# A gated decoder block on eight cores: token-major GLU into the convolution, LN statistics and pooling on VectorE, and small stages run beside the dense matmuls

## The chip, the cores and the metric

One Trainium2 chip, all 8 cores. Each core computes 2048 of the 4 x 4096 tokens, plus a halo of 32 earlier tokens, with all the weights; no core talks to another. The metric is the device time of the slowest core, in microseconds (us). Five engines matter: TensorE (PE, matmuls and transposes), VectorE (DVE), ScalarE (ACT), GpSimd (POOL) and SyncE (SP, which here only starts loads and stores). In the traces of this case each engine works through its own list of instructions in the order of the program: one that waits holds up everything behind it on that engine (in the changed kernel GpSimd stood 20.59 us before one load, and the load behind it was issued only after that). TensorE's results land in PSUM, which the kernels use as eight banks of 512 columns; VectorE or ScalarE reads them out (an eviction) before the kernel uses a bank again, and PE waits where that is late. In a matmul, the stationary operand is the one loaded into the array first (PEld in the views, 98 ns a load in the changed kernel's MLP). L-numbers are lines of the kernel; many are lines of helpers.

There is a second, slower state: in five executions here the cores of one die show a mean granted TensorE clock of 0.81 to 0.95 where the other die has 0.97 to 0.99, and the run is 7 to 15% longer. Such runs are left out. The experiments were run in several sessions and on several chips: there, the median of the fast runs of the kernel before was between 1136 and 1140.4 us, so differences of 3 us between two kernels of different sessions mean little.

## The reference, cut to what matters

```python
u = rms_norm(h, mix_pre_g)
proj = u @ w_in                               # 1024 -> 5120: a, gate, p, two gates
a, gate = split(proj[..., :2048])
c = depthwise_causal_conv(a * sigmoid(gate))  # 31 positions, per channel
c = swish(layer_norm(c))                      # over the 1024 channels of a token
y_conv = c @ w_conv_out
z = trailing_mean(p, windows 2, 4, 8, 16) - p # one window per group of 256 channels
y_pool = (einsum(z, pool_w) * pool_scale) @ w_pool_out
h = h + rms_norm((g_conv * y_conv + g_pool * y_pool) @ w_o, mix_post_g)
v = square(relu(rms_norm(h, mlp_pre_g) @ w_ff1)) @ w_ff2       # 1024 -> 4096 -> 1024
out = h + rms_norm(v, mlp_post_g)
```

The dense products (GLU, pool projection, gated products, w_o, MLP) fill TensorE. The rest, that is norms, convolution, LN and pooling, is small, but the dense products depend on it.

## The kernel before

Every stage is finished before the next one begins. The convolution is done on TensorE, on groups of 8 channels by 16 positions, so the channel-major GLU result has to be transposed, regrouped, transposed again, multiplied and transposed back. LN sums are matmuls with a matrix of ones. The trailing means are matmuls with band matrices.

```python
def glu_group(cc, t0, n, blk):                 # channel-major: weights stationary
    for (po, sl, ...) in (a-half, gate-half):
        for kc in range(8):
            MM(po, sl[:, kc, ccl*128:(ccl+1)*128], uT[:, kc, t0:t0+n], kc == 0, kc == 7, ...)
    ACT(tmpA, pg, AF.Sigmoid, ...)
    TTOP("dve", u[:, cc, t0:t0+n], pa, tmpA, ALU.mult, ...)
# ... cut ...
for step in range(8 + 3):                      # the conv, a stage of its own
    if 0 <= step - 1 < 8: cv_t2(step - 1)      # second transposes + PSUM eviction
    if step < 8:          cv_t1(step)          # first transposes, also of the halo
    if 0 <= step - 3 < 8: cv_t3(step - 3)      # back to channel-major
    if 0 <= step - 2 < 8: cv_mm(step - 2)      # the 31 taps; then loads the next taps
# ... cut ...
for cc in range(8):                            # LN sums: ones-matmuls of s and s*s
    MM(ps[:, blk, :], onesb[:], s_t[:, cc, ...], ...)
    MM(ps[:, 4 + blk, :], onesb[:], sqb[:, sb, ...], ...)
# ... cut: pooling by band matrices pmb, then pool_w, then the two gated passes ...
for j in range(16):                            # w_o, a stage of its own
    ctx = s5_a(j)                              # load x again, 16 matmuls, squares
    if pend is not None: s5_b(*pend)           # residual, store, norm for the MLP
    pend = (j, ctx)
```

Of the kernel before, what the change touches and what calls it, by code (L numbers as in the profile page):

```python
# [10 lines left out]
AX = mybir.AxisListType  # L11

H = 32
NT = 2048
# [7 lines left out]
OFF_RA, RA_N = 0, 8 * TT  # L22
OFF_RB, RB_N = OFF_RA + RA_N, 8 * TT
OFF_RD, RD_N = OFF_RB + RB_N, 8 * NT
OFF_RW, RW_N = OFF_RD + RD_N, 8 * 2048
OFF_RC, RC_N = OFF_RW + RW_N, 8192
OFF_RDM, RDM_N = OFF_RC + RC_N, 8192
ARENA_N = OFF_RDM + RDM_N

class KB:  # L30
    ENG = ("pe", "act", "dve", "pool", "sp")
    N_DMA_SEM = 16

    def __init__(self, nc):
        self.nc = nc
        self.q = {e: [] for e in self.ENG}
        self.count = {e: 0 for e in self.ENG}
        self.last_write = {}
        self.readers = {}
        self.waited = {e: {} for e in self.ENG}  # L40
        self.dma_val = [0] * self.N_DMA_SEM
        self.dma_next = 0
        self.n_sw = 0
        self.ranges = {}

    def reg(self, name, start, n):
        self.ranges[name] = (start, start + n)
# [10 lines left out]
    def _clobbers(self, w):  # L58
        rg = self.ranges.get(w)
        if rg is None:  # L60
            return ()
        out = []
        for n2, (s2, e2) in self.ranges.items():
            if n2 != w and s2 < rg[1] and rg[0] < e2 and (n2 in self.last_write or n2 in self.readers):
                out.append(n2)
        return out

    def op(self, eng, fn, reads=(), writes=(), dma=False, after=()):
# [3 lines left out]
        writes = list(writes)  # L72
        extra = []
        for w in writes:
            extra.extend(self._clobbers(w))
        for r in reads:
            ev = self.last_write.get(r)
            if ev is not None:
                self._need(eng, ev, waits)
            if isinstance(r, tuple) and r[0] == "ps":  # L80
                for ev in self.readers.get(r, ()):
                    if ev[0] != eng:
                        self._need(eng, ev, waits)
        for w in writes + extra:
            ev = self.last_write.get(w)
            if ev is not None:
                self._need(eng, ev, waits)
            for ev in self.readers.get(w, ()):
                self._need(eng, ev, waits)
# [14 lines left out]
        for w in writes:  # L104
            self.last_write[w] = ev
            self.readers[w] = []
        for w in extra:
            self.last_write.pop(w, None)
            self.readers.pop(w, None)
        for r in reads:  # L110
            self.readers.setdefault(r, []).append(ev)
        return ev

    def final_wait(self, eng, resources):
        waits = {}
        for r in resources:
            ev = self.last_write.get(r)
            if ev is not None:
                self._need(eng, ev, waits)
        self.q[eng].append((waits, None, None, False))  # L120
# [28 lines left out]
def build_program(dbg=None):  # L149
# [8 lines left out]
    pool_w = din("pool_w", [4, 256, 256])  # L158
# [4 lines left out]
    vecs = din("vecs", [128, 32 + 248])  # L163
    gbd = din("gb", [4, DM])
    identd = din("ident", [128, 128])
    pmd = din("pm", [128, 4 * 288])
    convw = din("convw", [8, 128, 16 * 3 * 128])
    out = nc.dram_tensor("out", [NT, DM], F32, kind="ExternalOutput").ap()
    dbg_cv = nc.dram_tensor("dbg_cv", [128, 8 * NT], BF16, kind="ExternalOutput").ap() if dbg == "cv" else None

    with ExitStack() as es:
        T = lambda name, shape, dt: es.enter_context(nc.sbuf_tensor(name, shape, dt))
        arena = T("arena", [128, ARENA_N], BF16)
        xt = T("xt", [128, 2, DM], F32)
        xb = T("xb", [128, 3, DM], BF16)
        gb = T("gbt", [128, 2, DM], F32)
        tmpA = T("tmpA", [128, 4, 512], F32)
        stat = T("stat", [128, 4, 512], F32)
        sm = T("sm", [128, 64], F32)
        epst = T("epst", [128, 2], F32)  # L180
        vec = T("vec", [128, 32 + 248], F32)
        identf = T("identf", [128, 128], F32)
        identb = T("identb", [128, 128], BF16)
        onesb = T("onesb", [128, 128], BF16)
        pmb = T("pmb", [128, 4, 288], BF16)
        junkb = T("junkb", [128, DM], BF16)
        ps = es.enter_context(nc.psum_tensor("ps", [128, 8, 512], F32))
        kb = KB(nc)

        def aview(off, cnt, **dims):  # L190
            v = arena[:, off:off + cnt]
            if dims:
                names = list(dims)
                pat = "p (" + " ".join(names) + ") -> p " + " ".join(names)
                v = v.rearrange(pat, **{k: dims[k] for k in names[:-1]})
            return v

        uT = aview(OFF_RA, RA_N, k=8, t=TT)
        u = aview(OFF_RB, RB_N, k=8, t=TT)
        z_t = aview(OFF_RB, 8 * NT, k=8, t=NT)  # L200
        s_t = aview(OFF_RD, RD_N, k=8, t=NT)
        sqb = aview(OFF_RC, RC_N, b=2, t=NT * 2)
        Dm = aview(OFF_RDM, 2 * 31 * 128, b=2, j=31, q=128)
        m1 = aview(OFF_RC, RC_N + RDM_N, k=8, t=NT)
        ptm = aview(OFF_RC, 4 * 1024, b=4, n=1024)
        h1 = aview(OFF_RC, 16384, f=32, t=512)
        hT_all = stat[:].rearrange("p a n -> p (a n)").bitcast(BF16).rearrange("p (k t) -> p k t", k=8)

        def slot(i):
            return aview(OFF_RW + i * 2048, 2048, k=8, n=256)  # L210

        def wff1_off(c):
            return (OFF_RA + c * 4096) if c < 4 else (OFF_RD + (c - 4) * 4096)

        def wff1_blk(c):
            return aview(wff1_off(c), 4096, k=8, n=512)

        def wff2_off(f):
            return (OFF_RB + f * 1024) if f < 16 else (OFF_RW + (f - 16) * 1024)

        def wff2_fc(f):
            return aview(wff2_off(f), 1024)

        WO_SL = 0
        wo_t = aview(OFF_RW, 8192, h=2, k=8, n=512)

        for k in range(8):
            kb.reg(("uT", k, -1), OFF_RA + k * TT, H)
            for b in range(4):
                kb.reg(("uT", k, b), OFF_RA + k * TT + H + b * 512, 512)  # L230
            kb.reg(("u", k), OFF_RB + k * TT, TT)
            for b in range(4):
                kb.reg(("z", k, b), OFF_RB + k * NT + b * 512, 512)
            kb.reg(("s", k), OFF_RD + k * NT, NT)
            kb.reg(("m1", k), OFF_RC + k * NT, NT)
            kb.reg(("rw", k), OFF_RW + k * 2048, 2048)
            kb.reg(("wff1", k), wff1_off(k), 4096)
        for b in range(2):
            kb.reg(("sqb", b), OFF_RC + b * 4096, 4096)
            kb.reg(("Dm", b), OFF_RDM + b * 3968, 3968)  # L240
            kb.reg(("wo", b), OFF_RW + b * 4096, 4096)
        for b in range(4):
            kb.reg(("ptm", b), OFF_RC + b * 1024, 1024)
        for f in range(32):
            kb.reg(("wff2", f), wff2_off(f), 1024)
            kb.reg(("h1", f), OFF_RC + f * 512, 512)

        st = {"bank": 0, "k": 0, "alt": 0, "xi": 0, "ti": 0}

        def nb():  # L250
            b = st["bank"]
            st["bank"] = (b + 1) % 8
            return b

        def PSK(b):
            return ("ps", b)

        def alt():
            st["alt"] ^= 1
            return "act" if st["alt"] else "dve"  # L260

        def nti():
            st["ti"] = (st["ti"] + 1) % 4
            return st["ti"]

        def MM(out_ap, lhsT, rhs, start, stop, reads, writes):
            kb.op("pe", lambda e: e.matmul(out_ap, lhsT=lhsT, rhs=rhs, start=start, stop=stop), reads=reads, writes=writes)  # L267

        def TR(out_ap, in_ap, ident_ap, reads, writes):
            kb.op("pe", lambda e: e.transpose(out_ap, in_ap, ident_ap), reads=reads, writes=writes)  # L270

        def ACT(out_ap, in_ap, func, reads, writes, bias=None, scale=None, accum=None):
            kw = {}
            if bias is not None:
                kw["bias"] = bias
            if scale is not None:
                kw["scale"] = scale
            if accum is not None:
                kw["accum_out"] = accum
            kb.op("act", lambda e: e.activation(out=out_ap, in_=in_ap, func=func, **kw), reads=reads, writes=writes)  # L280

        def TTOP(eng, out_ap, in0, in1, op, reads, writes):
            kb.op(eng, lambda e: e.tensor_tensor(out=out_ap, in0=in0, in1=in1, op=op), reads=reads, writes=writes)  # L283

        def TS(eng, out_ap, in0, s1, op0, reads, writes):
            kb.op(eng, lambda e: e.tensor_scalar(out=out_ap, in0=in0, scalar1=s1, scalar2=None, op0=op0), reads=reads, writes=writes)
# [594 lines left out]
```

## Time and profile before

Three runs gave a median of 1137.19 us (1135.94 to 1138.77). The profiled execution spans 1134.0 us on its slowest core.

The page of the kernel before, parts 1 and 2: busy time of an engine with its share and instruction count, then PE's busy tenths in 40 equal slices of the span.

```profile
PE 1034.5 (91%) x6184; PEld 535.8 (47%) x6184; DVE 464.0 (41%) x696; ACT 380.0 (34%) x664; POOL 63.7 (6%) x76
...
PE   2999987788887999999997789999999999999997
```

PE looks 91% busy, but its low digits stand together: at the start, in slices 6 to 13 and in slices 22 to 24. A table of stretches makes this plain. The windows view of the kernel before, core 2; I chose the borders at the stages, and the columns are as the first line says (after the borders comes the length).

```profile
core 2: us, PE busy (x) PEld busy (x) DVE busy (x) ACT busy (x) POOL busy (x), PEclk, DMA share, GB/s
...
150.50:236.00 85.50, 65.08 (x1025) 61.02 (x1023) 47.22 (x69) 33.81 (x39) 6.93 (x11) 0.92 0.84 139
236.00:349.60 113.60, 93.80 (x864) 73.31 (x864) 89.86 (x119) 54.85 (x77) 5.89 (x7) 0.91 0.38 45
349.60:602.50 252.90, 251.73 (x1152) 113.08 (x1152) 73.32 (x107) 57.12 (x97) 38.03 (x39) 0.99 0.42 64
602.50:683.00 80.50, 59.70 (x272) 25.79 (x273) 42.80 (x76) 27.08 (x78) 0.00 (x0) 0.92 1.00 245
683.00:1127.00 444.00, 438.50 (x2096) 200.36 (x2096) 155.97 (x239) 124.11 (x246) 3.86 (x5) 1.00 0.25 69
```

| stretch (us) | stage | PE busy of | clock |
|---|---|---|---|
| 0 to 24.7 | start | 4.4 of 24.7 | 1.00 |
| 150.5 to 236 | conv | 65.1 of 85.5 | 0.92 |
| 236 to 349.6 | LN statistics, pool projection, pooling | 93.8 of 113.6 | 0.91 |
| 349.6 to 602.5 | products with `pool_w` (to about 366), both gated passes, the first four w_o tiles | 251.7 of 252.9 | 0.99 |
| 602.5 to 683 | the other w_o tiles, the first w_ff1 groups | 59.7 of 80.5 | 0.92 |
| 683 to 1127 | the rest of the MLP | 438.5 of 444.0 | 1.00 |

The gated products and the MLP leave almost nothing between matmuls (1.2 of 252.9 and 5.5 of 444.0 us): there, less matmul time is what is left to save, at 0.216 us per matmul of 512 columns. Conv, LN with pooling, and w_o wait, and their clock is lower as well (0.91 to 0.92). The waits view of the kernel before names what PE waited for (total us, number of waits, longest):

```profile
PE ps L267 <- ACT arena L280: 16.2, 8, 5.5
PE ps L270 <- DVE xb L289: 16.1, 10, 4.7
```

These are waits for PSUM evictions and transposes that wait for a norm; convolution weights that land late add 9.3 us.

### The profile page before, as it was taken

What the parts mean: (1) busy time and instruction counts of PE and PEld (TensorE: products, weight loads), DVE (VectorE), ACT (ScalarE), POOL (GpSimd) and SP (SyncE); (2) the same over time, 40 slices, a digit from 0 to 9 for tenths busy, and PEclk for the clock granted to TensorE, in tenths of its full rate; (3) what the DMA queues carried; (4) which work ended last, traced back from release to release, by engine and by line L of the source; (5) the groups of instructions that cost most, each with busy time, mean ns of one, the idle gap of its engine ahead of it and who ended that gap; (6) DMA issues with size and microseconds to landing.
All of it is one profiled execution on the core that took longest, in us unless ns stands there. A gap on an engine that the chain in (4) does not pass through costs nothing.

```text
span 1134.0 us, 17007 instructions; the slowest of 8 cores (1114.2 to 1134.0 us)
## 1 busy us (share of the span) xinstructions
PE 1034.5 (91%) x6184; PEld 535.8 (47%) x6184; DVE 464.0 (41%) x696; ACT 380.0 (34%) x664; POOL 63.7 (6%) x76
## 2 busy tenths in 40 slices
PE   2999987788887999999997789999999999999997
PEld 1454467647773444444443334444444444444443
DVE  3343245549796111232235456323332333234322
ACT  4677333314655211111124234222332233223211
POOL 2000000020000100122130001000000000000000
PEclk9999999889888999999999989999999999999999
DMA  9921079983007061193529998723102310131012
GB/s 204 161 67 57 1 120 165 164 104 47 1 1 130 8 85 21 28 147 36 87 22 217 233 260 189 138 82 99 43 1 65 109 51 1 56 112 38 1 55 75
DMA packets 60320, 98.71 MB, mean 87 GB/s; under 512 B 2480, under 2 KB 42672, under 8 KB 59216
## 3 DMA queue, kind: packets, MB, share of 16 engines
q0 software_dynamic: 46080, 46.96, 28.8%
q1 hardware_dynamic: 14160, 50.68, 13.5%
q8 instruction: 51, 0.84, 0.3%
q14 instruction: 29, 0.24, 0.1%
HBM read 127.81 MB, written 16.78 MB: 127 GB/s over the span
## 4 chain that ended last, share of the span: by engine, by line
PE 73%; DMA 14%; DVE 6%; ACT 3%; issue 3%; SPq 1%; POOL 0%; DVEq 0%; ACTq 0%; POOLq 0%
PE ps L267 70%; DMA arena<-xh 4%; DMA arena<-w_in 3%; DMA arena<-convw 3%; PE ps L270 3%; DMA xt<-xh 3%; DVE tmpA L283 2%; DVE gbt L293 1%; ACT arena L280 1%; DVE arena L299 1%; DMA xt<-out 1%; DVE xt L289 1%; DMA arena<-pool_w 1%; ACT junkb L280 1%; DVE arena L289 0%
## 5 line engine op out<-in xcount | busy, mean ns | idle before, releaser
L267 PE MATMUL ps<-arena 128*128 128x512 bf16 (+4 forms) x3936 | 732.4, 348 | 28.8 <-DMA arena<-convw 9.3
L267 PEld LDWEIGHTS ps<-arena 128*128 128x128 bf16 (+1 forms) x3936 | 364.9, 100 | 380.3 <-issue 45.5
L280 ACT ACTIVATE tmpA<-ps 128x512 f32<-128x512 f32 (+1 forms) x232 | 135.1, 583 | 354.1 <-PE ps L267 344.9
L267 PE MATMUL ps<-stat,arena 128*128 128x512 bf16 x1024 | 222.1, 379 | 8.9 <-ACT junkb L280 5.1
L267 PEld LDWEIGHTS ps<-stat,arena 128*128 128x128 bf16 x1024 | 99.6, 98 | 130.5 <-issue 11.4
L283 DVE TENSOR_TENSOR arena<-tmpA 128x512 bf16<-128x512 f32 x128 | 88.1, 692 | 113.9 <-ACT tmpA L280 113.8
L283 DVE TENSOR_TENSOR arena<-ps,tmpA 128x512 bf16<-128x512 f32 (+1 forms) x72 | 45.8, 636 | 146.6 <-ACT tmpA L280 141.6
L280 ACT ACTIVATE junkb<-ps 128x512 bf16<-128x512 f32 x64 | 37.9, 592 | 146.7 <-PE ps L267 93.6
L280 ACT ACTIVATE arena<-ps 128x512 bf16<-128x512 f32 (+5 forms) x71 | 50.9, 719 | 61.7 <-DVE arena L299 31.1
L283 DVE TENSOR_TENSOR tmpA<-ps,gbt 128x512 f32<-128x512 f32 x64 | 42.2, 686 | 61.6 <-ACT junkb L280 44.7
L293 DVE RECIPROCAL sm<-sm 128x1 f32<-128x1 f32 (+1 forms) x65 | 10.5, 161 | 115.8 <-ACT sm L280 115.8
L280 ACT ACT_TABLE_LOAD x32 | 41.1, 1283 | 46.6 <-DVE tmpA L283 14.6
L283 DVE TENSOR_TENSOR tmpA<-ps,tmpA 128x512 f32<-128x512 f32 x32 | 22.1, 692 | 75.6 <-ACT tmpA L280 75.6
L280 ACT ACTIVATE junkb<-xt 128x1024 bf16<-128x1024 f32 x26 | 27.4, 1053 | 68.7 <-DMA xt<-out 66.1
L270 PE MATMUL ps<-identb,xb 128*128 128x128 bf16 (+1 forms) x264 | 21.7, 230 | 30.3 <-DVE xb L289 16.1
L270 PE MATMUL ps<-identb,arena 128*128 128x128 bf16 (+2 forms) x640 | 39.1, 213 | 8.2 <-DVE arena L299 4.4
L299 DVE CAST arena<-ps 128x512 bf16<-128x512 f32 (+1 forms) x54 | 37.0, 686 | 13.9 <-PE ps L267 10.9
L270 PEld LDWEIGHTS ps<-identb,arena 128*128 128x128 bf16 (+2 forms) x640 | 35.2, 106 | 11.6 <-issue 9.5
L289 DVE SCALAR_TENSOR_TENSOR xt<-tmpA,sm,xt 128x1024 f32<-128x1024 f32 x24 | 30.8, 1285 | 14.4 <-DMA xt<-xh 11.1
L270 PEld LDWEIGHTS ps<-identb,xb 128*128 128x128 bf16 (+1 forms) x264 | 17.7, 103 | 40.0 <-issue 35.7
L289 DVE SCALAR_TENSOR_TENSOR xb<-xt,sm,gbt 128x1024 bf16<-128x1024 f32 x26 | 33.4, 1284 | 3.2 <-DVE sm L293 0.7
L299 DVE COPY arena<-ps 128x1024 bf16<-128x1024 bf16 (+2 forms) x46 | 27.8, 618 | 11.4 <-ACT arena L280 9.4
(44 smaller groups left out, 359.2 us busy)
## 6 DMA issues: line engine op xcount, KB each, us to landing
arena<-w_ff POOLq DMA_DIRECT2D x16, 1024.0 KB, 26.8
xt<-out SPq DMA_DIRECT2D x28, 512.0 KB, 4.0
arena<-convw POOLq DMA_DIRECT2D x8, 1536.0 KB, 14.3
out<-xt SPq DMA_DIRECT2D x24, 512.0 KB, 3.4
xt<-xh SPq DMA_DIRECT2D x20, 512.0 KB, 8.1
arena<-w_in POOLq DMA_DIRECT2D x20, 512.0 KB, 15.2
arena<-xh SPq DMA_DIRECT2D x12, 512.0 KB, 8.7
out<-arena SPq DMA_DIRECT2D x8, 512.0 KB, 6.8
```

Of the source, the lines that this page charges most:

```text
L267: kb.op("pe", lambda e: e.matmul(out_ap, lhsT=lhsT, rhs=rhs, start=start, stop=stop), reads=reads, writes=writes)
L270: kb.op("pe", lambda e: e.transpose(out_ap, in_ap, ident_ap), reads=reads, writes=writes)
L280: kb.op("act", lambda e: e.activation(out=out_ap, in_=in_ap, func=func, **kw), reads=reads, writes=writes)
L283: kb.op(eng, lambda e: e.tensor_tensor(out=out_ap, in0=in0, in1=in1, op=op), reads=reads, writes=writes)
L289: kb.op("dve", lambda e: e.scalar_tensor_tensor(out=out_ap, in0=in0, scalar=scalar, in1=in1, op0=op0, op1=op1), reads=reads, writes=writes)
L293: kb.op("dve", lambda e: e.reciprocal(out_ap, in_ap), reads=reads, writes=writes)
L299: kb.op(eng, lambda e: e.tensor_copy(out_ap, in_ap), reads=reads, writes=writes)
```

## The change

The intent is to remove TensorE work that only moves or sums data, and to hide the rest of the small stages behind dense matmuls.

1. GLU is computed token-major: activations are the stationary operand, read with a stride of 16 tokens, and the result falls out in the order that the convolution needs. The first conv transposes disappear.
2. LN statistics are taken by VectorE instructions on the token-major conv result. The trailing means are a VectorE difference or running-sum scan. `pool_w`, `pool_scale` and `w_pool_out` are multiplied into one matrix on the chip.
3. Order: pool projection first (its pooling runs in the background), then GLU in four quarters with the previous quarter's convolution in between, then the first gated pass with the last convolution, LN and the transposes back, then the second gated pass with the w_o tiles of finished token blocks; the last four w_o tiles go between the first w_ff1 groups.
4. Reciprocal square roots of w_o and LN move to GpSimd (add, then power −0.5), so that ScalarE need not switch tables (32 table loads before, of 1.28 us each).

The kernel is almost wholly rewritten; this is the diff cut to its core.

```diff
-def glu_group(cc, t0, n, blk): ...                        # channel-major
+def glu_pair(q, rp):                                      # token-major
+    for i in range(2):
+        r = 2 * rp + i
+        for k in range(8):
+            MM(ps[:, b + i, :], uT[:, k, H + r:H + NT:16], wg[q % 2][:, k, :, :]...., k == 0, k == 7)
 # ... cut ...
-for step in range(8 + 3): cv_t2 / cv_t1 / cv_t3 / cv_mm   # a stage of its own
+for blk in range(4):                                      # pool projection
+    if blk == 0:
+        p_halo()
+    for cc in range(8):
+        nxt = 4 * (blk + 1) + cc // 2
+        if cc % 2 == 0 and nxt < 16:
+            x_norm(nxt)            # ACT square + sqrt, DVE reciprocal + multiply
+        p_group(cc, blk)           # 8 matmuls, ACT eviction; queues a pool_task
+        if cc % 2 == 1 and nxt < 16:
+            x_tr(nxt)              # 8 transposes, eviction by ACT or DVE in turn
+        if cc % 2 == 1 or blk == 3:
+            pump(1)                # one queued pool_task on VectorE
+for q in range(4):                                        # GLU, conv of q-1 between
+    glu_halo(q)
+    steps = deque(conv_steps(q - 1) if q else [])
+    for rp in range(8):
+        glu_pair(q, rp)
+        pump(3)
+        if rp % 2 == 1 and steps:
+            steps.popleft()()      # ... a step of the conv; it loads the next taps
+    # ... cut: wg_load, weff_prep, weff_scale, LN statistics queued ...
+wload2(wgp, w_in_v[:, :, 4096:5120])                      # the first gate weight
+wload2(wco, wco_v)
 # ... cut: first gated pass with conv_steps(3), LN, cv_t3 ...
+def wo_tile(j):
+    # 16 matmuls into two PSUM banks
+    resid(b, gb1, 2, res, dst[:, 0:512], j, "pool")       # squares, rsqrt, residual, store
+    r = rstd(res, 128, 0, dst, "pool")                    # square, rsqrt
+    STT(dst, res, r, gb2, ALU.mult, ALU.mult)             # the norm for the MLP
 # ... cut ...
-for j in range(16): ctx = s5_a(j); ...                    # w_o, a stage of its own
+for blk in range(4):                                      # second gated pass
+    for cc in range(8):
+        gated(cc, blk, wco, s_t, wgc, False)
+        if blk and cc % 2 == 1:
+            wo_step()              # a w_o tile of the block before
+        elif blk and len(trq) > 1:
+            h_tr(trq.popleft())
+# w_ff1, first block: two ff1 groups, a w_o tile and the transposes of an earlier one
```

## The prediction

> **What bounds the kernel now.** TensorE is busy 1034.5 of 1134.0 us (page, part 1), but the busy time by stretches shows two kinds of stage. The gated products (349.6 to 602.5 us) and the MLP (683 to 1127) are full: PE busy 251.7 of 252.9 and 438.5 of 444.0, granted clock 0.99 to 1.00, one 128x512 matmul every 0.216 us. The others are bound by waits, not by TensorE: start and projection to 57.8 us, conv 150.5 to 236 (PE 65.1 of 85.5, clock 0.92; transposes wait for PSUM evictions and for convw, which lands in 14.3 us), LN statistics and pooling 236 to 349.6 (93.8 of 113.6; a 3.35 us reciprocal, table loads of 1.28, 8.8 us for pool_w), and w_o 602.5 to 683 (59.7 of 80.5, DMA share 1.00, x reloads).
>
> **What is removed.** Counting matmul columns: about 2.341 M before, 2.246 M after. Gone are the first conv transposes (main and halo, 33 k), the ones-matmuls of LN (33 k), the pooling bands (18 k), the pool halo's cost and half of pool_w (now folded, 16 k); GLU halo matmuls grow slightly. At 0.216 us per 512 columns: 40 us of PE. The larger part is waiting: the conv and pooling stages' chains now run beside GLU, gate and w_o matmuls.
>
> **Where the time lands, my sum (estimates from the durations above).** First dense matmul 34 (four w_in chunks; before, chunk pairs landed about every 8 us from 24.7); pool projection, transposes and halo 64; GLU 117.5, with conv matmuls 22 and folding 7, gives 146; first gate pass with the last conv pair and the output transposes 125; second gate pass with w_o 174; MLP 442; tail 8. Sum 993.
>
> **New waits, which I add.**
> 1. The first gate weight (2 MB as bf16) is issued on the POOL queue after the last convw (1.5 MB), and that one waits for the conv matmul ending the GLU stage. Both then land together; at the 140 to 190 GB/s seen for such loads, about 20 to 26 us. PE has 1.7 us of work first: stall about 22, plus about 2 for the clock afterwards ([...]here 32 matmuls after a 6.8 us gap took 9.9 instead of 6.9 us).
> 2. Second gate pass waits for the last Silu: 2.5.
> 3. w_o tiles: a DVE-POOL-ACT-DVE chain, estimated 10 us per 10.8 us of PE, is nearly critical; in the first w_ff1 groups (7.4 us of PE) it exceeds it: 7 together.
> 4. DVE pooling: 32 tasks [...]. It fits: 0 to 3.
> 5. Unmodelled gaps: 5.
>
> Total span about 1033, so **1036 us** measured; range **1012 to 1062**. Faster by over 2%: 0.96; within 2%: 0.03; slower: 0.01.
>
> **What would show it.** PE columns of 0.216 us and about 15 dense MLP us saved at most; one PE wait of about 20 us on w_in at the GLU-to-gate border (230 to 280 us); no long wait in the conv; PE busy near 950 to 970; VectorE busy up in share, off the chain of waits.
>
> **What would make it wrong.** GpSimd's pow on 128x1 taking over 1 us (each costs twice per w_o tile, so w_o would bind); the gate weight landing early or only with the following loads; strided weight reads in GLU slower than 0.216 us (the strided transposes of before kept 0.058, so I think not); VectorE falling behind in GLU; a throttled clock in the denser stages.

Two passages are cut from it, at the marks: in step 1 a rule about the clock, in step 4 the cost assumed for a pooling task. Neither was read from a trace of this case. No term of the sum goes with them: 993 and the new waits of 24 (22 + 2), 2.5, 7, 1.5 (the middle of step 4) and 5 make 1033.

## The result and the profile after

The changed kernel took 1086.37 us, median of 4 runs (1084.67 to 1088.38), against 1136.93 (1135.94 to 1138.77, 4 runs) for the kernel before on the same chip: a ratio of 0.9551 (0.9534 to 0.9569). Ratios here are the mean time of one kernel's fast runs over the mean of the other's in the same rounds, so they are not quite the ratio of the medians. The change is faster by 4.5%, and it gains half of the 101 us that were predicted. 1086 lies outside the predicted range.

The page of the changed kernel, parts 1 and 2 (94 of the 5136 matmul records are missing from this trace):

```profile
PE 972.8 (90%) x5042; PEld 488.0 (45%) x5136; DVE 424.6 (39%) x685; ACT 311.9 (29%) x565; POOL 62.6 (6%) x112
...
PE   1578999999199999999999679899999999999997
```

PE has some 62 us less to do (1034.5 to 972.8), but is only 90% busy: its idle time has not shrunk, it went from 99.5 to 111.5 us. So the whole gain of this change is work taken off TensorE; the waits that it removed were replaced by others. There are three holes: slices 1 to 4, slice 11, and slices 23 to 26. The windows view of the changed kernel, core 2, columns as before:

```profile
0.00:39.20 39.20, 6.56 (x104) 5.40 (x106) 8.62 (x21) 10.61 (x20) 7.37 (x12) 1.00 1.02 192
39.20:118.30 79.10, 65.26 (x339) 30.35 (x345) 54.28 (x96) 39.77 (x74) 0.56 (x1) 0.96 0.46 101
118.30:157.00 38.70, 36.09 (x156) 21.75 (x158) 27.45 (x39) 7.95 (x13) 2.30 (x3) 0.96 0.42 67
157.00:274.10 117.10, 115.83 (x812) 81.35 (x822) 42.99 (x62) 35.65 (x52) 7.24 (x11) 1.00 0.64 106
274.10:299.70 25.60, 0.03 (x1) 0.02 (x1) 0.00 (x0) 0.00 (x0) 1.31 (x2) 0.58 1.00 151
299.70:427.60 127.90, 127.18 (x756) 65.52 (x769) 44.31 (x84) 42.86 (x55) 4.96 (x4) 0.98 0.31 60
427.60:587.80 160.20, 157.31 (x771) 72.89 (x787) 87.78 (x130) 54.92 (x113) 22.97 (x50) 1.00 0.49 117
587.80:647.40 59.60, 41.78 (x197) 19.11 (x200) 27.25 (x41) 19.04 (x39) 13.03 (x27) 0.88 0.60 131
...
693.70:1076.30 382.60, 380.73 (x1729) 173.01 (x1764) 113.28 (x186) 84.33 (x174) 0.00 (x0) 1.00 0.12 42
```

The stages with much work in them are as full as the change meant them to be: three GLU quarters with convolution and folding at 115.8 of 117.1 us, the first gated pass at 127.2 of 127.9, the second with w_o at 157.3 of 160.2. The lost time is in three stretches: the pool projection (39.2 to 118.3), an idle gap of 25.6 us in front of the gates, and the last four w_o tiles in the first w_ff1 groups (from 587.8). The waits view of the changed kernel:

```profile
PE ps L220 <- DMA arena<-w_in: 33.8, 3, 25.6
PE ps L223 <- DVE arena L250: 29.4, 16, 5.5
...
PE ps L220 <- DMA arena<-w_ff: 4.0, 2, 3.7
```

The waits of before on convolution weights and on pooling weights are gone. What is there now: one load of `w_in` (25.6 us), and 16 waits of transposes (L223) for a VectorE multiply (L250), which is the last step of a norm: 4 of them at the start (6.6 us), 8 in the pool projection (9.5 us) and 4 in the last w_o tiles (13.3 us). Here is the whole miss, term by term, my sum beside the span:

| part | predicted | measured | difference |
|---|---|---|---|
| to the first dense matmul | 34 | 39.2 | +5.2 |
| pool projection, transposes, halo | 64 | 79.1 | +15.1 |
| GLU, conv, folding (with step 4, middle 1.5) | 147.5 | 155.8 | +8.3 |
| wait for the gate weight (predicted: with the clock after it; measured: without, it lies in the next row) | 24 | 25.6 | +1.6 |
| first gated pass | 125 | 127.9 | +2.9 |
| second gated pass, w_o, MLP (174 + 442 + 2.5 + 7) | 625.5 | 648.7 | +23.2 |
| tail | 8 | 8.0 | 0 |
| gaps | 5 | 0 | −5 |
| sum | 1033 | 1084.3 | +51 |

Two lines hold most of it. Note that the wait for the gate weight is the largest single wait, but not a part of the miss: the prediction had counted 24 us for it.

Another view of the same numbers. Before, from the products with `pool_w` (349.6 us) to the end of the MLP (1127) it is 777.4 us; after, from the first gate products (299.7) to the end of the MLP (1076.3) it is 776.6 us. The two stretches do not hold the same work: the first has the `pool_w` products, the second has the last quarter of the convolution and the transposes back. But PE is busy for 749.9 us in the first and 749.0 us in the second, so it is idle for 27.5 us in both. The change gained everything it gained in front of this border, and behind it no idle time, although the w_o stage (80.5 us at 74% busy) had been dissolved there.

### The pool projection: a ring over three engines

The timeline of the changed kernel around two transposes of the pool projection, core 2. Columns: start, duration, engine, line, instruction, count, and in brackets the idle time before it and what ended it.

```profile
48.88 0.61 PE L223 MATMUL ps<-identb,arena 128*128 128x128 bf16 x8 [0.70 <-DVE arena L250]
...
49.59 1.02 ACT L238 ACTIVATE arena<-ps 128x1024 bf16<-128x1024 bf16 x1 [0.71 <-PE ps L223]
50.51 1.05 ACT L238 ACTIVATE arena<-arena 128x1024 bf16<-128x1024 f32 x1
...
52.14 0.16 DVE L374 RECIPROCAL sm<-sm 128x1 f32<-128x1 f32 x1 [2.14 <-ACT sm L238]
52.42 1.28 DVE L250 SCALAR_TENSOR_TENSOR arena<-arena,sm 128x1024 bf16<-128x1024 f32 x1
...
53.96 0.61 PE L223 MATMUL ps<-identb,arena 128*128 128x128 bf16 x8 [1.02 <-DVE arena L250]
```

Read it as a circle. The transposes of tile j (48.88) are copied out by ScalarE (49.59). Only then, because it stands behind the copy in ScalarE's program, does the square of tile j+1 start (50.51). Its root, the reciprocal (52.14) and the multiply (52.42) follow, and the transposes of j+1 (53.96) wait for that. One turn takes 5.1 us (48.88 to 53.96). TensorE has 4.0 us of work in a turn, ScalarE 4.2 us. Data of tile j and tile j+1 do not depend on each other; program order on ScalarE and on TensorE ties them into a ring.

This is every second turn. ScalarE and VectorE make the copy in turn, and when VectorE makes it (54.67), ScalarE has the square of the next tile done early, but VectorE does not take up the norm: behind the copy stands a pooling task. The timeline of the next turn, same core:

```profile
55.28 1.48 DVE L241 TENSOR_TENSOR arena<-arena 128x514 f32<-128x514 f32 x2
...
57.86 0.16 DVE L374 RECIPROCAL sm<-sm 128x1 f32<-128x1 f32 x1
...
59.69 0.61 PE L223 MATMUL ps<-identb,arena 128*128 128x128 bf16 x8 [1.67 <-DVE arena L250]
```

The square root was ready at 55.06; the reciprocal came at 57.86, after the pooling task. In the whole stage, turns of the first kind cost 3.0 us of waiting (three waits of 1.0), turns of the second kind 6.5 us (0.70, 1.67, 1.38, 1.48, 1.28), and the borders of the blocks 3.8 us (three waits of 1.3 for the last copy). I call both kinds ring 1: in both, the norm of the next tile stands behind other work in program order.

### The gate weight

The timeline of the changed kernel at the border of GLU and gates, lines of POOL and PE:

```profile
272.94 0.53 POOL L262 DMA_DIRECT2D arena<-convw  x1 [20.59 <-PE ps L220]
273.63 0.90 POOL L262 DMA_DIRECT2D arena<-w_in  x1 [0.17 <-issue]
...
299.71 3.57 PE L220 MATMUL ps<-arena 128*128 128x512 bf16 x8 [25.58 <-DMA arena<-w_in]
```

GpSimd starts all weight loads. The load of the last convolution taps needs a buffer that PE reads until 272.9, so GpSimd stood there for 20.59 us, and the gate weight behind it (2 MB as bf16, 4 MB in memory) was issued at 273.6, when PE was about to need it. The eight matmuls after the gap took 3.57 us in place of 1.73: the granted clock was 0.58 in the gap and 0.50 in those 3.57 us.

### The last w_o tiles: a second ring

The timeline of the changed kernel in the first w_ff1 groups, one turn, core 2:

```profile
600.55 0.16 DVE L241 TENSOR_TENSOR sm<-sm 128x1 f32<-128x1 f32 x1 [2.95 <-ACT arena L238]
600.87 0.22 POOL L369 TENSOR_SCALAR sm<-sm 128x1 f32<-128x1 f32 x1 [5.94 <-DVE sm L241]
601.24 0.57 POOL L370 TENSOR_TENSOR sm<-sm,mhalf 128x1 f32<-128x1 f32 x1
601.91 0.76 DVE L250 SCALAR_TENSOR_TENSOR ps<-ps,sm,arena 128x512 f32<-128x512 f32 x1 [1.20 <-POOL sm L370]
...
605.20 1.06 ACT L238 ACTIVATE arena<-arena 128x1024 bf16<-128x1024 f32 x1 [4.75 <-DVE arena L241]
...
607.62 1.28 DVE L250 SCALAR_TENSOR_TENSOR arena<-arena,sm 128x1024 bf16<-128x1024 f32 x1 [2.62 <-POOL sm L370]
608.82 1.29 DVE L246 TENSOR_SCALAR ps<-ps 128x512 f32<-128x512 f32 x2
609.61 2.49 ACT L238 ACTIVATE arena<-ps 128x512 bf16<-128x512 f32 x4 [3.25 <-DVE ps L246]
...
613.06 0.16 DVE L241 TENSOR_TENSOR sm<-sm 128x1 f32<-128x1 f32 x1 [2.95 <-ACT arena L238]
```

VectorE adds the two sums of squares (600.55), GpSimd makes the reciprocal root (600.87 to 601.8), VectorE multiplies and adds the residual to 605.0, ScalarE squares the new h (605.20), GpSimd again, VectorE norms (607.62). Only then does VectorE reach the ReLU of the two w_ff1 groups (608.82), which stand behind the whole chain in its program. ScalarE squares them (609.61) and only behind that the next w_o tile, whose sums are added at 613.06. A turn takes 12.51 us and contains 7.4 us of matmuls at full clock (two w_ff1 groups of 1.73, a w_o tile of 3.46 and the transposes of 0.45). The windows view of exactly this turn:

```profile
600.55:613.06 12.51, 8.08 (x36) 3.44 (x35) 5.46 (x8) 4.41 (x9) 2.53 (x5) 0.86 0.44 90
```

No engine is full: PE is busy 8.1 us of 12.5 (part of it at a lowered clock), VectorE 5.5, ScalarE 4.4, GpSimd 2.5.

### The profile page after: what moved, and what is told of

The parts are those of the page before. It is cut to its first block, busy times and chain, and to the rows that moved or that the text cites. A ratio compares the mean times of both kernels' runs of the same rounds, so it can differ in the third digit from the quotient of the medians.

```text
span 1084.3 us, 14235 instructions; the slowest of 8 cores (1072.2 to 1084.3 us)
## 1 busy us (share of the span) xinstructions
PE 972.8 (90%) x5042; PEld 488.0 (45%) x5136; DVE 424.6 (39%) x685; ACT 311.9 (29%) x565; POOL 62.6 (6%) x112
## 4 chain that ended last, share of the span: by engine, by line
PE 75%; DMA 9%; DVE 6%; issue 4%; ACT 3%; POOL 1%; DVEq 0%; ACTq 0%; SPq 0%; POOLq 0%
PE ps L220 72%; DMA arena<-w_in 5%; DMA arena<-w_ff 4%; ACT arena L238 3%; PE ps L223 2%; DVE arena L250 2%; DVE arena L241 2%; DVE arena L436 1%; DVE ps L250 1%; DMA arena<-xh 1%; POOL arena L262 1%; POOL sm L370 1%; DVE ps L246 0%; DVE arena L256 0%; POOL sm L369 0%
## 5 line engine op out<-in xcount | busy, mean ns | idle before, releaser
L220 PE MATMUL ps<-arena 128*128 128x512 bf16 (+2 forms) x4514 | 941.2, 367 | 57.1 <-DMA arena<-w_in 33.8
L220 PEld LDWEIGHTS ps<-arena 128*128 128x128 bf16 x4608 | 453.8, 104 | 525.9 <-issue 81.8
L238 ACT ACTIVATE arena<-ps 128x512 bf16<-128x512 f32 (+5 forms) x382 | 237.4, 638 | 655.6 <-PE ps L220 469.5
L246 DVE TENSOR_SCALAR ps<-ps 128x512 f32<-128x512 f32 x128 | 88.2, 698 | 108.4 <-PE ps L220 108.4
L241 DVE TENSOR_TENSOR arena<-ps,arena 128x512 f32<-128x512 f32 (+3 forms) x116 | 87.0, 755 | 92.9 <-ACT arena L238 61.8
L250 DVE SCALAR_TENSOR_TENSOR arena<-arena,ps 128x512 bf16<-128x512 f32 (+1 forms) x64 | 43.9, 685 | 127.5 <-ACT arena L238 72.1
L223 PE MATMUL ps<-identb,arena 128*128 128x128 bf16 (+1 forms) x520 | 40.4, 230 | 46.4 <-DVE arena L250 29.4
L223 PEld LDWEIGHTS ps<-identb,arena 128*128 128x128 bf16 (+1 forms) x520 | 34.7, 103 | 61.0 <-issue 54.5
L250 DVE SCALAR_TENSOR_TENSOR arena<-arena,sm 128x1024 bf16<-128x1024 f32 (+1 forms) x33 | 42.4, 1284 | 43.4 <-POOL sm L370 41.5
L250 DVE SCALAR_TENSOR_TENSOR ps<-ps,sm,arena 128x512 f32<-128x512 f32 x64 | 48.3, 754 | 21.0 <-POOL sm L370 19.4
L241 DVE TENSOR_TENSOR arena<-arena 128x512 bf16<-128x512 f32 (+2 forms) x56 | 38.4, 690 | 4.2
L262 POOL DMA_DIRECT2D arena<-w_in x14 | 12.5, 920 | 87.6 <-PE ps L220 76.8
L250 DVE SCALAR_TENSOR_TENSOR arena<-arena 128x512 bf16<-128x512 f32 x24 | 16.5, 687 | 1.3
```

What stands on the lines that cost most here:

```text
L220: kb.op("pe", lambda e: e.matmul(o, lhsT=l, rhs=r, start=start, stop=stop), [l, r], [o])
L223: kb.op("pe", lambda e: e.transpose(o, i, idn), [i, idn], [o])
L238: kb.op("act", lambda e: e.activation(out=o, in_=i, func=func, **kw), rd, wr)
L241: kb.op(eng, lambda e: e.tensor_tensor(out=o, in0=a, in1=b, op=op), [a, b], [o])
L246: kb.op("dve", lambda e: e.tensor_scalar(out=o, in0=a, scalar1=s1, scalar2=s2, op0=op0, **kw), rd, [o])
L250: kb.op("dve", lambda e: e.scalar_tensor_tensor(out=o, in0=a, scalar=s, in1=b, op0=op0, op1=op1), rd, [o])
```

## The experiments

The theory: three separate waits of TensorE hold most of its new idle time, namely ring 1 in the pool projection, the order of issue on the GpSimd queue, and ring 2 in the last w_o tiles. (The two rings are parts of the miss; the second wait had been predicted.) Rivals: VectorE is simply too busy with pooling in stage 1 (then its work counts, not the order); the gate weight is bound by the memory's rate and its wait would only move; and in ring 2 GpSimd's power instruction and the two hops to GpSimd are at fault. Nine kernels were made from the changed one and run; all gave correct results.

| kernel | median us (of fast runs) | ratio to before | runs |
|---|---|---|---|
| changed kernel | 1086.37 | 0.9551 | 4 |
| gate weight loaded early | 1059.88 | 0.9307 | 4 |
| norm one tile ahead | 1074.27 | 0.9438 | 3 fast, 1 slow |
| pooling tasks late | 1090.45 | one look | 1 |
| w_o tile in three parts | 1073.98 | 0.9436 | 4 |
| rsqrt of the last w_o tiles on ScalarE | 1080.72 | one look | 1 |
| the first, second and fourth together | 1033.52 | 0.9096 | 4 |
| five further changes of order | 1017.13 | 0.8961 | 4 |
| first w_ff2 block in halves | 1011.83 | 0.8879 | 3 fast, 1 slow |
| PSUM bank reset after it | 1001.13 | 0.8795 | 4 |

### Experiment 1: the gate weight issued before the last convolution taps

```diff
             if q == 2:
                 weff_scale()
+                WLOAD(wgp, w_in_v[:, :, 4096:5120])
 ...
-        wload2(wgp, w_in_v[:, :, 4096:5120])
         wload2(wco, wco_v)
```

> One edit of the changed kernel: the 2 MB gate weight is put on the POOL queue one GLU quarter earlier (after the weight scaling, ahead of the last two convw loads). Theory: the 25.6 us wait on w_in at 274 us is only queue order. The wait falls below 2 us, no other PE wait grows by over 3 us, time about 1059 us. Rival: the queue is simply full there (DMA share 1.00), so the wait moves to a later convw or w_conv_out load: time above 1072 us.

Measured: 1059.88 us (1057.90 to 1060.35), ratio 0.9307 (0.9277 to 0.9337), 26.5 us less than the changed kernel. The timeline at the border, from the last GLU matmuls on, core 2:

```profile
259.30 14.99 PE L220 MATMUL ps<-arena 128*128 128x512 bf16 x104
274.13 1.06 PE L223 MATMUL ps<-identb,arena 128*128 128x128 bf16 x16
```

There is no bracket, so no wait: the first gate matmuls lie inside these lines, and PE is busy for all of the 17 us from 259 to 276 at a clock of 0.9 or more (PEclk 9 in the page of this run). Of the gain only about 1.6 us came back, as a longer wait for `w_ff` later (1.97 and 3.65 us in place of 0.35 and 3.70). The wait was one of order of issue, not of the memory's rate.

### Experiment 2: the norm one tile ahead

```diff
+        x_norm(4)
         for blk in range(4):
 ...
-                if cc % 2 == 0 and nxt < 16:
-                    x_norm(nxt)
+                if cc % 2 == 0 and nxt + 1 < 16:
+                    x_norm(nxt + 1)
```

Work, engines and instructions stay the same; only the norm of tile j+1 now stands one turn earlier, so its square is ahead of the copy of tile j on ScalarE, and its reciprocal and multiply are no longer awaited at once on VectorE.

> One edit of the changed kernel: the RMS norm of an x tile is emitted one tile ahead of its transposes. Theory: the pool projection stage (39.2 to 118.3 us, 79 us against 60 us of PE work) is bound by a loop of latencies: uT copy on ACT 1.0, square 1.05+0.19, sqrt 0.3, reciprocal, norm 1.28 on DVE, transposes 0.6, copy again. Taken apart, the stage takes 61 to 66 us; some of it is given back by a VectorE backlog in the first GLU quarter (2.4 us wait there now, up to 8). Time 1068 to 1075. Rival: VectorE has too much work with the pooling tasks; then the stage stays above 74 us and the time above 1081.

Measured: 1074.27 us (median of three fast runs, 1073.82 to 1074.61; one run of 1202.74 us is left out), ratio 0.9438 (0.9393 to 0.9483), 12.1 us less. The timeline of PE in the pool projection, core 5:

```profile
61.40 0.61 PE L223 MATMUL ps<-identb,arena 128*128 128x128 bf16 x8
...
65.30 0.61 PE L223 MATMUL ps<-identb,arena 128*128 128x128 bf16 x8
...
75.13 3.61 PE L220 MATMUL ps<-arena 128*128 128x512 bf16 x16 [1.41 <-DVE arena L250]
```

The transposes no longer wait: a turn is 3.90 us (61.40 to 65.30), all of it PE's. What is left is 1.41 us at each of three block borders, where the copy of the block's last tile is awaited. The stage takes 67.2 us (38.9 to 106.1) in place of 79.1, a little over what I had expected (61 to 66), and nothing of it is given back in the GLU stage. The same VectorE and ScalarE work fits in 67 us, so ring 1 was order and latency, not load.

### Experiment 3: the pooling tasks late

```diff
-                if cc % 2 == 1 or blk == 3:
+                if blk == 3:
                     pump(1)
```

> One edit of the changed kernel, to split the cause of the same 79 us stage: no pooling task runs in its first three quarters; all of them come later. Rival (the pooling tasks in VectorE's queue are the cause): the stage falls to 60 to 63 us. Theory (a loop of latencies that exists without them, of which they lengthen every second turn): it falls only to 68 to 72 us. Either way the first GLU quarter gets longer by the moved tasks, so the whole time says little.

Measured: one look, 1090.45 us. The stage took 70.8 us (38.1 to 108.9), as the theory had it. Of the eight waits of transposes four are left: three of 1.0 us, one in each block, in turns in which ScalarE makes the copy, and one of 0.31 us; the three block borders still take 1.31 us each. For instance in the timeline of core 6:

```profile
52.50 0.61 PE L223 MATMUL ps<-identb,arena 128*128 128x128 bf16 x8 [1.01 <-DVE arena L250]
```

Without any pooling on VectorE in three of the four blocks, the first kind of turn still holds PE up, and the second kind does not. So the pooling tasks account for about 8 of the 15 us (79.1 to 70.8), by standing ahead of the norm in VectorE's program as shown above; the rival was a good half of it. But the work has to be done, and the GLU stage then waited for VectorE for 4.95, 1.27 and 5.51 us. Moving the work away is no gain, and moving the norm ahead removes both kinds of wait with the pooling left where it is.

### Experiment 4: the w_o tile in three parts

Each part of the chain is put behind one more dense group in program order, so that the evictions of that group stand ahead of it.

```diff
 def wo_tile(j):
     # 16 matmuls
-    resid(b, gb1, 2, res, dst[:, 0:512], j, "pool")
-    r = rstd(res, 128, 0, dst, "pool")
-    STT(dst, res, r, gb2, ALU.mult, ALU.mult)
+    r1 = resid_sq(b, 2, dst[:, 0:512], "pool")      # squares, sum, rsqrt: at once
+    def part_b():                                   # residual, store, square, rsqrt
+        resid_add(b, gb1, r1, res, j)
+        hold.append(rstd(res, 128, 0, dst, "pool"))
+    def part_c():                                   # the norm; then j may be transposed
+        STT(dst, res, hold[0], gb2, ALU.mult, ALU.mult)
+        trq.append(j)
+    dfr.append(part_b)
+    dfr.append(part_c)                              # one taken from dfr after each dense group
```

With it, a tile may be transposed as soon as its norm is out (`elif trq` in place of `len(trq) > 1`), and the reload of x moves into the last part.

> One edit of the changed kernel: a w_o tile's work after its matmuls is cut in three parts, each emitted one matmul group later, so that VectorE no longer waits in order for POOL and ACT. Theory: the four w_o tiles among the first w_ff1 groups turn at 12.5 us each, a serial loop DVE-ACT-DVE-POOL-DVE-ACT-POOL-DVE, where PE has 7.4 us of work. The stretch from 588 us to the last w_ff1 group of the first block falls from 97.5 to 76 to 82 us; the wait for w_ff after it grows from 4 to at most 10 us. Time 1068 to 1076. Rival: the engines' work itself is too much there; then the turn stays above 11 us and the time above 1081.

Measured: 1073.98 us (1072.86 to 1076.01), ratio 0.9436 (0.9405 to 0.9467), 12.4 us less. The timeline of PE in the same place, core 2:

```profile
599.64 0.61 PE L223 MATMUL ps<-identb,arena 128*128 128x128 bf16 x8 [0.66 <-DVE arena L250]
...
608.29 0.61 PE L223 MATMUL ps<-identb,arena 128*128 128x128 bf16 x8 [1.14 <-DVE arena L250]
```

and the windows view of this turn:

```profile
599.64:608.29 8.65, 7.51 (x40) 3.51 (x41) 5.51 (x8) 4.40 (x10) 2.53 (x5) 1.00 0.86 129
```

The turn is 8.65 us in place of 12.51 with the same busy time on VectorE, ScalarE and GpSimd (5.5, 4.4, 2.5 us). From the start of the second gated pass to the last transposes of h it is 204.5 us in place of 217.8. The one expectation that missed is the length of the stretch from 588 us on: about 84 us where I had written 76 to 82. 1.14 us per turn of ring 2 is left, and the last transposes still wait 4.18 us.

### Experiment 5: no GpSimd in the last w_o tiles

```diff
-            resid(b, gb1, 2, res, dst[:, 0:512], j, "pool")
-            r = rstd(res, 128, 0, dst, "pool")
+            resid(b, gb1, 2, res, dst[:, 0:512], j, "pool" if j < 12 else "act")
+            r = rstd(res, 128, 0, dst, "pool" if j < 12 else "act")
```

> One edit of the changed kernel: the four w_o tiles among the first w_ff1 groups take 1/sqrt from ACT's Sqrt and VectorE's reciprocal in place of GpSimd's add and pow. Theory (the turn of 12.5 us is the sum of a serial loop; GpSimd's two parts of about 1.2 and 1.0 us with their hops are only a fifth of it): the turn falls by about 1 us to 11.3 to 11.8 us, the whole by some 4 us. Rival (GpSimd's pow, 0.57 us, is what makes w_o bind, as the prediction feared): the turn falls to about 8 us and the whole by 15 us or more.

Measured: one look, 1080.72 us. The timeline of VectorE, the sums of two neighbouring turns:

```profile
615.15 0.16 DVE L241 TENSOR_TENSOR sm<-sm 128x1 f32<-128x1 f32 x1 [2.96 <-ACT arena L238]
...
627.10 0.16 DVE L241 TENSOR_TENSOR sm<-sm 128x1 f32<-128x1 f32 x1 [2.96 <-ACT arena L238]
```

The turns are 12.94 (with a table load), 11.95 and 11.67 us, against 12.51. With GpSimd out of the ring it is hardly shorter, so the power instruction is not what makes a turn long. The root on ScalarE and the reciprocal on VectorE, which took its place, have hops of their own (in the turns without a table load VectorE waited 0.55 us for the first root, where it had waited 1.20 us for GpSimd), so this run alone does not show what a ring without hops would take. That the place of the chain in the program counts is shown by experiment 4.

### Experiment 6: do the three add up?

The edits of experiments 1, 2 and 4 together, nothing else.

> The edits of e1, e2 and e4 together, nothing else. Theory: three separate waits of TensorE, so the gains add: 26.5 + 12 + 12.4 us, time 1033 to 1040. Rival: they share something (HBM or the DMA queue during the loads, VectorE's backlog, the granted clock), and 10 us or more are given back elsewhere: time above 1045.

Measured: 1033.52 us (1032.73 to 1036.06), ratio 0.9096 (0.9069 to 0.9123). The single gains are 26.5, 12.1 and 12.4 us, together 51.0, which from 1086.4 gives 1035.4. They add, to 2 us: three waits in three different stretches. That 1033.5 us is close to the predicted 1036 is luck. The prediction had counted the wait for the gate weight (24 us), which is gone here. Without it, the two rings account for 24.5 of the 50 us of the miss; the other half is spread over the later start (5.2), the GLU stage (8.3), the first gated pass (2.9), what is left of the two rings' stretches (3 and 11) and smaller terms.

### Experiments 7 to 9: what the waits left, and a better version

Experiment 7 adds five further changes of order to experiment 6; they were not tried one by one. In words, not code:

```text
+ halo of the pool projection by pairs of column groups, as each weight chunk lands
+ transposes x_tr one group earlier (even cc); pooling tasks at every group in blocks 2 and 3
+ all loads of w_ff that have room queued when the second gated pass ends
+ a w_o tile at every third w_ff1 group (not every second), the last part one group later
+ the last transposes of h from the 16th w_ff1 group on
```

> e6 with what its traces suggest next: pool halo by weight chunk, so that the first dense matmuls start at 29 and not 39 us (about 6 us), x transposes one group earlier (3 block borders of 1.4 us), w_ff loads queued together when the gate pass ends (4 to 5 us), w_o tiles every third w_ff1 group and the last h transposes later (about 8 us), pooling tasks spread more evenly (2 to 4 us). Expected 1014 to 1024 us; if the startup is bound by HBM and not by the order of the halo, about 6 us more.

Measured: 1017.13 us (1016.13 to 1024.82), ratio 0.8961 (0.8923 to 0.8998), within the 1014 to 1024 expected. The pool projection keeps one wait, of 0.89 us. A new limit shows in the timeline of core 5:

```profile
615.39 3.57 PE L220 MATMUL ps<-arena 128*128 128x512 bf16 x8 [11.22 <-DMA arena<-w_ff]
```

Now that PE arrives earlier, the weights of the second MLP product are late. From 525 us to the end of this wait the DMA share was 1.00, with 182 GB/s: so here it seems to be the rate of the loads, not their order of issue; no run tried another order.

Experiment 8 lets the first block of w_ff2 run over the half of the weights that has landed, for all four tiles, and then over the other half; this holds all eight PSUM banks.

```diff
+            if blk == 0:
+                for h in range(2):                  # halves of the w_ff2 rows, in order of landing
+                    for tl in range(4):
+                        for hh in range(2):
+                            for n in range(16 * h, 16 * h + 16):
+                                MM(ps[:, 2 * tl + hh, :], ..., n == 0, n == 31)
+                        if h:
+                            resid(2 * tl, gb3, ...)
+                continue
```

> e7, and in the first block only, w_ff2 runs over the first half of its weights for all four token tiles before it needs the second half. e7's trace shows what is left at this border: 12.6 us of PE waiting for w_ff while the DMA engines are 0.98 busy, 10 MB asked for after the gate pass and landing at about 178 GB/s. Theory (the loads are now the limit there, and PE has other work that it could do): 27.6 us of matmuls come before the last weights are needed, the wait goes below 2 us, time 1004 to 1009 us. Rival: the tiles' residual work, now bunched, blocks the PSUM banks of the next block and gives back 5 us or more: above 1011.

Measured: 1011.65, 1011.83 and 1014.21 us in fast runs, ratio 0.8879 (0.8848 to 0.8909); a fourth run, 1078.85 us, was slow. The expected 1004 to 1009 us was missed, and the rival that had been written down came in its place. The wait for `w_ff` is gone, and another stands there (timeline, core 2):

```profile
668.17 333.84 PE L220 MATMUL ps<-arena 128*128 128x512 bf16 x1506 [8.28 <-DVE arena L241]
```

The next block's first group was given the PSUM banks of the last tile, whose residual was still under way, waiting 3.30 us itself for a late load of its rows of `out`. Experiment 9 starts again at the bank that had been free longest:

```diff
                         if h:
                             resid(2 * tl, gb3, 0, xres[tl % 2], hT[0][:, 0, :], tl, "act")
+                st["bank"] = 0
                 continue
```

> One line more than e8. e8 lost 8.3 us of its gain to a new wait: the second block's first w_ff1 group is given the PSUM bank of the last tile, whose residual waits for a late load of its row block. Here that block starts again at bank 0, free for 20 us by then. Theory: this wait is only the choice of bank; it goes below 1 us, time 1003 to 1007 us. Rival: VectorE's in-order queue (the tile's residual stands before the group's relu) holds the group anyway: the wait moves to the following banks and the time stays above 1009.

Measured: 1001.13 us (1000.37 to 1004.83), ratio 0.8795 (0.8770 to 0.8821), a little better than the 1003 to 1007 expected: the wait was the choice of bank. This beats both kernels, the changed one by 85 us. Its page, part 1 (all matmul records are present):

```profile
PE 961.0 (96%) x5136; PEld 483.3 (48%) x5136; DVE 423.2 (42%) x685; ACT 311.9 (31%) x568; POOL 62.6 (6%) x112
```

VectorE, ScalarE and GpSimd are busy for the same time as in the changed kernel (423.2 and 424.6, 311.9 and 311.9, 62.6 and 62.6 us). Every gain from 1086 to 1001 came from order, and in the last step from the choice of PSUM bank. PE's longest wait is now the start, 17.4 us.

## Why the prediction was right or wrong

The direction was right, the size was wrong: 101 us predicted, 51 measured.

**Right.** The count of TensorE work: PE's busy time fell to 972.8 us, a little over the 950 to 970 that had been written, and to 961.0 in experiment 9. The waits of the conv and of the LN and pooling stages are gone, as said. Step 1 of the new waits read the border right in cause and nearly in size: "The first gate weight … is issued on the POOL queue after the last convw", 22 plus 2 us predicted, 25.6 us of wait and 1.8 us of slow clock measured, and experiment 1 shows it. (That this was called inevitable in the sum, and not a fault to be mended by one moved line, is another matter.) GpSimd's power on 128x1 took 0.57 us, below the 1 us that was feared (the add before it took 0.22 us; on 128x16, in LN, the power took 2.94 us). Strided reads of the stationary operand did not slow the matmuls: in experiment 2's first GLU quarter 128 matmuls follow one another in 27.78 us without a wait, 0.217 us each. The strided weight loads themselves took 145 ns in the changed kernel (124 to 157 us), against 98 ns in its MLP, but beside the matmuls. The clock was not throttled in the denser stages: it was 0.98 to 1.00 in the GLU quarters from 157 us on, in the gated passes and in the MLP. A core's mean was 0.968 to 0.978 in the fast runs of the changed kernel, whose clock was low in stretches with waits (0.58 in the gap, 0.88 in the last w_o tiles), and 0.997 to 0.999 in experiment 9.

**Wrong, the first step that failed: "pool projection, transposes and halo 64".** This is PE's work, and I took PE's work as the stage's length, because each of the other engines had room in it. Each had: VectorE was busy 54.3 and ScalarE 39.8 us of 79.1. But the norm of the next tile stood behind the copy of this one, on ScalarE in one turn and, with a pooling task too, on VectorE in the next, and most turns took 5.1 to 5.7 us where PE needed 4.0. The stage came to 79.1 us, 15.1 over the sum; experiment 2 takes 11.9 of them away by moving one line of program order. The first dense matmul came 5.2 us late, too: the halo matmuls stand first in the program and need all four weight chunks (PE waits 2.7 and 5.5 us for `w_in` between them). Experiment 7 changes that, among other things, and there dense matmuls begin at about 28 us, against 39; its share in the gain was not measured alone.

**Wrong, the second: step 3, "in the first w_ff1 groups (7.4 us of PE) it exceeds it: 7 together".** The mechanism was right, and was named; the size was not. I costed the chain of a w_o tile alone, at 10 us. In the program the ReLU and squares of two w_ff1 groups stand inside the ring, behind the chain and ahead of the next tile's squares, so a turn is 12.51 us: 5.1 us over PE's work and not 2.6. In the stretch from 587.8 to 647.4 us, PE is busy 41.8 of 59.6 us at a clock of 0.88: about 18 us of idle time and a few more by the clock, where 7 had been written. Waiting for `w_ff`, which the sum did not have, added 4 us. The chain "estimated 10 us per 10.8 us of PE, is nearly critical" in the second gated pass held: PE is at 157.3 of 160.2 us there.

**Wrong, smaller: step 4, "It fits: 0 to 3".** The GLU stage with all in it is 8.3 us over the sum (6.8 over the top of this range's 149). One wait for VectorE of 2.4 us at the end of the first quarter and a clock of 0.96 to 157 us are seen; the rest of the 8 us was not pursued. The scan took 1.25 us for 528 columns where an add of 512 took 0.69, and pooling tasks with a scan follow one another every 2.24 us (106.67 and 108.91 us). "VectorE busy up in share" was wrong as well: 41% became 39%, since the change also took copies and casts out of PSUM away from it (its two largest groups of them took 56 us before; 5.5 us are left).

**Where the gain went.** In front of the border the change gained 50 us (349.6 to 299.7): PE has 61 us less to do there, partly because some 15 us of convolution and transposes moved behind it, and is idle for 11 us more, with 25.6 us of the new wait and 15 of ring 1. Behind the border no idle time was gained: w_o's 21 us (80.5 less 59.7) came back as the 18 us of ring 2's stretch and the 4 us of waiting for `w_ff`.

## What to carry to other kernels

When a small stage is interleaved with a dense one, cost the turn of the ring and not the work of each engine: walk one tile through every in-order engine, and count what stands ahead of it in each program, including the other stage's instructions. The sign in a profile is a short wait that comes back at every tile while no engine is full (in ring 2 a turn of 12.51 us with PE busy for 8.1 and VectorE for 5.5), and the remedy that worked here (experiments 2 and 4) is to start the next tile's chain ahead of this tile's last step or to spread a chain over several dense groups (8.65 us a turn, with no buffer added). Where one engine issues all loads, as GpSimd does here, look for a load whose buffer is still in use: here it stood for 20.59 us with the gate weight behind it, and PE then waited 25.58 us; to issue first what had room gained 26.5 us.
